# Mean over 8192 rows: paired loads up to row group 61, no early loads, the last group in pieces of 8, 4, 3 and 1 blocks, and 57 products on TensorE

## The chip, the cores and the metric

The kernel runs on one core of one Trainium2 chip. The metric is device time in microseconds (us): 628.41 us before the change, the median of three runs that lie between 628.18 and 628.45 us.

## The reference

```python
x = np.random.randn(8192, 8192).astype(np.float32)
return np.mean(x, axis=0)
```

The input is 8192 rows of 8192 floats, 268.4 MB in HBM. The result is one row of 8192 column means, 32 KB. Every input element is read once and enters one sum.

## The kernel before

**Tiling.** 128 rows make a row group (`G` = 64 groups, numbered 0 to 63), one row to a partition, 4 MB each. A row group has 16 blocks of `F` = 512 columns. One SBUF tile, `bufs`, holds six row groups: four are targets of loads, the fifth (`both`) and the sixth (`acc`) are used by the additions. Adding two row groups element by element keeps the 128 partial sums of a column apart, on 128 partitions; at the end TensorE sums over the partitions.

**Loading.** SyncE issues all loads (line 76), in program order, on one DMA queue. The first two loads of rows fetch groups 0 to 3 and 4 to 5; from group 6 to group 55 a load fetches two groups, so that each partition receives two neighbouring rows, 64 KB. From group 56 on a load fetches one group, 32 KB to a partition. A load into a buffer waits for the VectorE addition that read the buffer last. Two loads go ahead of their place (lines 111 and 113): blocks 14 and 15 of group 60 and blocks 9 to 13 of group 63 go to a tile of their own, `early`. GpSimd adds them into `acc` while the main loop runs (line 129), and the later loads of groups 60 and 63 leave these blocks out.

**Adding.** `add` (line 94) gives an addition to VectorE. Where an addition needs both a load and the addition before it, a no-op on ScalarE or GpSimd waits for the two, and the addition waits for the no-op. In the main loop there are two additions for a load: the pair is summed into `both`, and `both` is added to `acc`. Groups 56 to 59 are added to `acc` one by one. Of group 60 only blocks 0 to 13 are added on VectorE, of group 61 blocks 7 to 15. Three blocks of group 62 (14, 15 and 8) are added to `acc` by GpSimd (line 148).

**Summing over the partitions.** A product (line 183) multiplies a 128 x 32 tile filled with 1/8192 with a block of columns and accumulates in PSUM. It uses one of four 32-column parts of the TensorE array (`tile_position`, `q` = 0 to 3), so four products with different `q` can run side by side. What VectorE and GpSimd did not add goes to TensorE: blocks 0 to 6 of group 61, blocks 0 to 13 except 8 of group 62, and the 11 blocks of group 63 that were not loaded early, beside the 16 blocks of `acc`. With blocks that are spread over the four parts in pieces of 128, 160, 256 or 512 columns this makes 63 products. The order of the list `sums` is the order on TensorE.

**The end.** ScalarE copies four PSUM tiles to SBUF, VectorE copies the last one, and five stores write the result: two issued by ScalarE, three by SyncE. `landed` puts waits on SyncE; in the version before, they stand behind the last store.

What sets the order: each engine executes its own instructions in program order; engines wait for each other and for DMAs by semaphores.

Of the kernel before, what the change touches and what calls it, by code (L numbers as in the profile page):

```python
# [9 lines left out]
def kernel(  # L10
# [2 lines left out]
    x: bass.AP,  # L13
    out: bass.AP,
):

    nc = tc.nc
    f32 = mybir.dt.float32
    M, N = x.shape  # L40
    P = nc.NUM_PARTITIONS
    F = 512
    W = F // 4
    G = M // P
    U = 6
    sync = mybir.DependencyInfo(mybir.DependencyClass.Sync, mybir.DependencyReason.DATA)

    sb = ctx.enter_context(tc.tile_pool(name="sb", bufs=1))
    psp = ctx.enter_context(tc.tile_pool(name="psum", bufs=1, space=bass.MemoryType.PSUM))
# [2 lines left out]
    both = bufs[:, U - 2, :]  # L52
    acc = bufs[:, U - 1, :]
    ones = sb.tile([P, 32], f32, name="ones")
    early = sb.tile([P, 7 * F], f32, name="early")
    tail = sb.tile([P, W], f32, name="tail")
    warm = sb.tile([P, 32], f32, name="warm")
    nc.gpsimd.memset(ones[:], 1.0 / M)  # L58
    ready = sb.tile([P, 1], f32, name="ready")
    tc.keep_in_program_order(  # L60
        nc.gpsimd.tensor_add(out=ready[:], in0=ones[:, 0:1], in1=ones[:, 1:2]))  # L61
    banks = [psp.tile([P, F], f32, name=f"bank{b}") for b in range(2)]
    wide = psp.tile([P, 2 * F], f32, name="wide")
    two = psp.tile([P, 2 * W], f32, name="two")
    last = psp.tile([P, W], f32, name="last")

    loads = []

    def landed(*inss):

        nop = tc.keep_in_program_order(nc.sync.nop()).ins
        for o in inss:
            tc.add_manual_dep(nop, o.name, sync, reason="SyncE waits")

    def load(dst, src):
        ins = tc.keep_in_program_order(nc.sync.dma_start(out=dst, in_=src)).ins  # L76
        k = len(loads)
        over = loads[k - 8:k - 6] if k >= 8 and k % 2 == 0 else []
        tc.declare_no_dep(ins, group="loads", keep=over, reason="the reader of the buffer waited")
        for o in over:  # L80
            tc.add_manual_dep(ins, o.name, sync, reason="covers the next load too")
        tc.add_to_no_dep_group("loads", ins)
        loads.append(ins)
        return ins

    def rows(g, n=1):
        return x[g * P:(g + n) * P, :]

    def load_rows(g, u, n):
        return load(bufs[:, u:u + n, :], rows(g, n).rearrange("(p j) c -> p j c", j=n))  # L90
# [2 lines left out]

    def add(dst, a, b, dmas):

        ins = nc.vector.tensor_add(out=dst, in0=a, in1=b).ins  # L96
        if dmas and adds:
            waiter = nc.scalar if len(adds) % 8 > 1 else nc.gpsimd
            nop = joins[waiter] = tc.keep_in_program_order(waiter.nop()).ins  # L99
            for o in dmas + adds[-1:]:  # L100
                tc.add_manual_dep(nop, o.name, sync, reason="the no-op waits")
            for group in ("loads", "adds"):
                tc.declare_no_dep(ins, group=group, reason="the no-op waited")
            tc.add_manual_dep(ins, nop.name, sync, reason="waits for both at once")
        elif adds:
            tc.declare_no_dep(ins, group="loads", reason="the add ahead waited")
        tc.declare_no_dep(ins, group="early", reason="the no-op waited, or the add behind it")
        tc.add_to_no_dep_group("adds", ins)
        adds.append(ins)

    load(early[:, 5 * F:], rows(G - 4)[:, 14 * F:])
    first, second = load_rows(0, 0, 4), load_rows(4, 4, 2)
    load(early[:, :5 * F], rows(G - 1)[:, 9 * F:14 * F])
    add(bufs[:, 2:4, :], bufs[:, 2:4, :], bufs[:, 0:2, :], [first])
    add(bufs[:, 4:6, :], bufs[:, 4:6, :], bufs[:, 2:4, :], [second])
    add(acc, acc, both, [])
    tc.keep_in_program_order(nc.scalar.copy(out=warm[:], in_=ones[:]))  # L117
    ahead = []
    g = 6
    while g < G - 8:  # L120
        u = (g + 2) % 4
        dma = load_rows(g, u, 2)
        add(both, bufs[:, u, :], bufs[:, u + 1, :], [dma])
        add(acc, acc, both, ahead)
        ahead = []
        if g in (24, 32):
            lo, hi = (0, 4) if g == 24 else (4, 7)
            cols = slice((9 + lo) * F, (9 + hi) * F)
            ins = tc.keep_in_program_order(nc.gpsimd.tensor_add(  # L129
                out=acc[:, cols], in0=acc[:, cols], in1=early[:, lo * F:hi * F])).ins  # L130
            tc.add_to_no_dep_group("early", ins)
            ahead = [ins]
        g += 2

    while g < G - 4:
        row = bufs[:, (g + 2) % 4, :]
        add(acc, acc, row, [load(row, rows(g))])
        g += 1
    for lo, hi, loaded in [(0, 14, 14), (7, 16, 16)]:
        row = bufs[:, (g + 2) % 4, :]  # L140
        dma = load(row[:, :loaded * F], rows(g)[:, :loaded * F])
        cols = slice(lo * F, hi * F)
        add(acc[:, cols], acc[:, cols], row[:, cols], [dma])
        g += 1
    r61, r62, r63 = [bufs[:, (g + 1 + j) % 4, :] for j in range(3)]
    load(r62, rows(g))
    for cols in [slice(14 * F, 16 * F), slice(8 * F, 9 * F)]:
        joined = tc.keep_in_program_order(nc.gpsimd.tensor_add(  # L148
            out=acc[:, cols], in0=acc[:, cols], in1=r62[:, cols])).ins
    g += 1  # L150
    for lo, hi in [(4, 8), (0, 4), (14, 16), (8, 9)]:
        load(r63[:, lo * F:hi * F], rows(g)[:, lo * F:hi * F])

    sums = []

    def blocks(row, lo, hi):
        for i in range(lo, hi):
            sums.append((banks[i // 4], i % 4, 0, row[:, i * F:(i + 1) * F]))

    def spread(dst, row, lo, hi, part=slice(None)):  # L160
        n = (hi - lo) * W
        for c in range(0, n, F)[part]:
            for q in range(4):
                at = lo * F + q * n + c
                sums.append((dst, q, c, row[:, at:at + min(F, n - c)]))

    blocks(acc, 2, 5)
    blocks(acc, 0, 2)
    blocks(r61, 0, 7)
    blocks(acc, 5, 8)  # L170
    blocks(r62, 0, 8)
    spread(wide, acc, 9, 14, slice(1))
    blocks(r63, 4, 8)
    spread(wide, r62, 9, 14, slice(1))
    for row in (acc, r62):
        spread(wide, row, 9, 14, slice(1, 2))
    spread(two, acc, 14, 16)
    blocks(r63, 0, 4)
    spread(last, acc, 8, 9)
    spread(two, r63, 14, 16)  # L180
    spread(last, r63, 8, 9)
    for n, (dst, q, c, cols) in enumerate(sums):
        summed = tc.keep_in_program_order(nc.tensor.matmul(  # L183
            out=dst[32 * q:32 * q + 32, c:c + cols.shape[1]],
            lhsT=ones[:],
            rhs=cols,
            start=all((d is dst, k, at) != (True, q, c) for d, k, at, _ in sums[:n]),
            stop=all((d is dst, k, at) != (True, q, c) for d, k, at, _ in sums[n + 1:]),
            tile_position=(0, 32 * q),
            skip_group_check=True,  # L190
        )).ins

    res = both[:, :2 * F].rearrange("p (b c) -> p b c", b=2)
    res5 = both[:, 2 * F:2 * F + 5 * W]
    res2 = both[:, 4 * F:4 * F + 2 * W]

    def copy(dst, src):
        return tc.keep_in_program_order(nc.scalar.copy(out=dst, in_=src)).ins  # L198

    def store(engine, dst, src, *then):  # L200
        ins = tc.keep_in_program_order(engine.dma_start(out=dst, in_=src)).ins
        for o in then:
            tc.add_manual_dep(ins, o.name, sync, reason="follows that load")
        return ins

    def part(lo, hi):
        return out[lo * F:hi * F].rearrange("(q c) -> q c", q=4)

    copy(res[:, 1, :], banks[1][:])
    s1 = store(nc.scalar, part(4, 8), res[0:P:32, 1, :], loads[-4])  # L210
    copy(res5, wide[:, :5 * W])
    copy(res[:, 0, :], banks[0][:])
    copied = copy(res2, two[:])
    ended = nc.vector.tensor_copy(out=tail[:], in_=last[:]).ins  # L214
    landed(*joins.values())
    s5 = store(nc.sync, part(9, 14), res5[0:P:32, :], *loads[-7:-3])
    s0 = store(nc.sync, part(0, 4), res[0:P:32, 0, :])
    s2 = store(nc.scalar, part(14, 16), res2[0:P:32, :])
    store(nc.sync, part(8, 9), tail[0:P:32, :])
    landed(loads[-2], joined)  # L220
    landed(loads[-1], copied)
    landed(s0, s5)
    landed(s1, summed)
    landed(s2, ended)
    hold = tc.keep_in_program_order(nc.vector.nop()).ins
    tc.add_manual_dep(hold, s0.name, sync, reason="VectorE ends late")

# [29 lines left out]
```

## Time and profile before

| | |
|---|---|
| median of three runs | 628.41 us |
| span of the profiled execution, first to last instruction | 626.4 us |
| VectorE busy | 529.3 us (85%), 60 instructions |
| TensorE busy | 13.3 us (2%), 126 records for 63 products |
| GpSimd busy | 12.0 us (2%) |
| ScalarE busy | 3.7 us (1%) |
| HBM read | 268.44 MB, 429 GB/s over the span |

For the profiled execution only the span is given; its device time is taken to be the span plus 2.0 us, so that it stands at the median of the runs shown.

The profile has engine rows (PE is TensorE, PEld its weight loads, DVE is VectorE, ACT is ScalarE, POOL is GpSimd, SP is SyncE). An engine name with a q, such as SPq, is that engine's sequencer, which issues DMAs and waits. A line "out<-in" names what is written and read. [...]

### The profile page before, as it was taken

To read this page: it belongs to the slowest core of one execution; us is meant where nothing else is said; L and a number is where in the kernel's file an instruction comes from. 1 tells how busy PE (TensorE), PEld (TensorE's weight loads), DVE (VectorE), ACT (ScalarE), POOL (GpSimd) and SP (SyncE) were. 2 spreads that over 40 slices of the span, in tenths; PEclk is the share of its full clock that TensorE was granted. 3 is DMA by queue.
4 is the path that set the end of the run, shared out by engine and by line. 5 is a ranking of instruction groups with operands and counts; after the bars stand their busy time and mean duration, and the time that the engine had idled before them with its cause. 6 is when DMAs were issued, how large, how long until landed. Compare 5 with 4: busy or idle time off the path is not lost.

```text
span 626.4 us, 484 instructions
## 1 busy us (share of the span) xinstructions
PE 13.3 (2%) x126; PEld 4.0 (1%) x126; DVE 529.3 (85%) x60; ACT 3.7 (1%) x6; POOL 12.0 (2%) x10
## 2 busy tenths in 40 slices
PE   0000000000000000000000000000000000000008
PEld 0000000000000000000000000000000000000002
DVE  0028999998888998889998899888898888999992
ACT  0000000000000000000000000000000000000001
POOL 0000000000000000020000200000000000000002
PEclk9999999999999999999999999999999999999999
DMA  8999999999999999999999999999999999999997
GB/s 372 465 402 428 459 410 460 402 469 402 469 402 469 402 469 402 469 402 469 402 465 406 439 431 427 444 410 460 402 469 402 469 402 469 402 435 435 419 435 305
DMA packets 5930, 268.50 MB, mean 429 GB/s; under 512 B 660, under 2 KB 668, under 8 KB 1064
## 3 DMA queue, kind: packets, MB, share of 16 engines
q1 hardware_dynamic: 5912, 268.46, 99.3%
q8 instruction: 1, 0.02, 0.0%
q10 hardware_dynamic: 16, 0.01, 0.0%
q14 instruction: 1, 0.01, 0.0%
HBM read 268.44 MB, written 0.03 MB: 429 GB/s over the span
## 4 chain that ended last, share of the span: by engine, by line
DMA 59%; DVE 30%; another core or an unknown queue 10%; issue 0%; SPq 0%; ACTq 0%; PE 0%; POOL 0%; POOLq 0%
DMA bufs<-in_x_dram 59%; DVE bufs L96 30%; SPq L76 0%; ACTq L99 0%; PE last L183 0%; DVE tail L214 0%; POOL ready L61 0%; POOL ones L58 0%; POOLq L99 0%; POOLq L241 0%
## 5 line engine op out<-in xcount | busy, mean ns | idle before, releaser
L96 DVE TENSOR_TENSOR bufs<-bufs 128x8192 f32<-128x8192 f32 (+3 forms) x59 | 529.0, 8966 | 85.9 <-DMA bufs<-in_x_dram 43.0
L183 PE MATMUL bank<-bufs,ones 128*32 128x512 f32 x62 | 10.0, 716 | 610.3 <-DVE bufs L96 610.0
L129 POOL TENSOR_TENSOR bufs<-bufs,early 128x2048 f32<-128x2048 f32 (+1 forms) x2 | 7.9, 3954 | 348.5 <-DVE bufs L96 348.5
L148 POOL TENSOR_TENSOR bufs<-bufs 128x1024 f32<-128x1024 f32 (+1 forms) x2 | 3.6, 1824 | 258.9 <-DMA bufs<-in_x_dram 258.9
L214 DVE COPY tail<-last 128x128 f32<-128x128 f32 x1 | 0.3, 291 | 8.8 <-PE last L183 8.8
L183 PEld LDWEIGHTS bank<-bufs,ones 128*32 128x32 f32 x62 | 2.2, 121 | 616.4 <-issue 614.5
L198 ACT COPY bufs<-bank 128x512 f32<-128x512 f32 x2 | 1.2, 586 | 617.9 <-PE bank L183 617.9
L183 PE MATMUL wide<-bufs,ones 128*32 128x512 f32 (+1 forms) x32 | 2.5, 432 | 0.0
L117 ACT ACT_TABLE_LOAD x1 | 1.3, 1283 | 0.7 <-PEq L241 0.7
L183 PE MATMUL two<-bufs,ones 128*32 128x256 f32 x16 | 1.2, 380 | 0.0
L183 PEld LDWEIGHTS wide<-bufs,ones 128*32 128x32 f32 x32 | 1.0, 110 | 1.8 <-issue 1.8
L183 PE MATMUL last<-bufs,ones 128*32 128x128 f32 x16 | 0.8, 279 | 0.1
L198 ACT COPY bufs<-wide 128x640 f32<-128x640 f32 x1 | 0.7, 692 | 1.1 <-PE wide L183 1.1
L183 PEld LDWEIGHTS last<-bufs,ones 128*32 128x32 f32 x16 | 0.4, 109 | 1.2 <-issue 0.6
L183 PEld LDWEIGHTS two<-bufs,ones 128*32 128x32 f32 x16 | 0.4, 109 | 0.1
L198 ACT COPY bufs<-two 128x256 f32<-128x256 f32 x1 | 0.4, 372 | 0.1
L117 ACT COPY warm<-ones 128x32 f32<-128x32 f32 x1 | 0.2, 217 | 0.0
L61 POOL TENSOR_TENSOR ready<-ones 128x1 f32<-128x1 f32 x1 | 0.2, 193 | 0.1
L58 POOL MEMSET ones<- 128x32 f32 x1 | 0.1, 125 | 0.3 <-POOLq L241 0.3
L241 POOL MEMSET const-float32-0.0<- 128x1 f32 x1 | 0.1, 98 | 0.2 <-issue 0.2
L241 POOL MEMSET const-bfloat16-1.0<- 128x1 bf16 x1 | 0.1, 102 | 0.0
L241 POOL MEMSET const-uint8-127<- 128x1 uint8 x1 | 0.1, 102 | 0.0
(1 smaller groups left out, 0.1 us busy)
## 6 DMA issues: line engine op xcount, KB each, us to landing
bufs<-in_x_dram SPq DMA_DIRECT2D x6, 4096.0 KB, 20.4
bufs<-in_x_dram SPq DMA_DIRECT2D x1, 3584.0 KB
bufs<-in_x_dram SPq DMA_DIRECT2D x2, 1024.0 KB, 18.7
early<-in_x_dram SPq DMA_DIRECT2D x1, 1280.0 KB
early<-in_x_dram SPq DMA_DIRECT2D x1, 512.0 KB
bufs<-in_x_dram SPq DMA_DIRECT2D x1, 512.0 KB, 19.4
bufs<-in_x_dram SPq DMA_DIRECT2D x27, 29.9
bufs<-in_x_dram SPq DMA_DIRECT2D x1, 256.0 KB, 19.7
```

The source lines that it names most:

```text
L58: nc.gpsimd.memset(ones[:], 1.0 / M)
L61: nc.gpsimd.tensor_add(out=ready[:], in0=ones[:, 0:1], in1=ones[:, 1:2]))
L96: ins = nc.vector.tensor_add(out=dst, in0=a, in1=b).ins
L117: tc.keep_in_program_order(nc.scalar.copy(out=warm[:], in_=ones[:]))
L129: ins = tc.keep_in_program_order(nc.gpsimd.tensor_add(out=acc[:, cols], in0=acc[:, cols], in1=early[:, lo * F:hi * F])).ins
L148: joined = tc.keep_in_program_order(nc.gpsimd.tensor_add(out=acc[:, cols], in0=acc[:, cols], in1=r62[:, cols])).ins
L183: summed = tc.keep_in_program_order(nc.tensor.matmul(out=dst[32 * q:32 * q + 32, c:c + cols.shape[1]], lhsT=ones[:], rhs=cols, start=all(( ...
L198: return tc.keep_in_program_order(nc.scalar.copy(out=dst, in_=src)).ins
L214: ended = nc.vector.tensor_copy(out=tail[:], in_=last[:]).ins
L241: nc = _bacc.Bacc("TRN2", target_bir_lowering=False, num_devices=1)
```

## The change

The two early loads and their tile go, and with them the two GpSimd additions in the main loop. The first load now fetches groups 0 and 1, straight into `both` and `acc`, and every load up to that of groups 60 and 61 fetches two groups: 31 loads of 8 MB. Groups 60 and 61 are added to `acc` whole, by six VectorE additions over blocks 0 to 7, 8 to 11 and 12 to 15. Groups 62 and 63 are not added by VectorE or GpSimd at all: TensorE sums them. Group 62 is one load; group 63 comes in four loads of 8, 4, 3 and 1 blocks. TensorE makes 57 products: for `acc`, group 62 and group 63 each 15 of 512 columns, and the block 15 of each is spread over the four parts in pieces of 128 columns. ScalarE makes four copies (the fourth of 96 partitions), VectorE copies the last tile. There are three stores: blocks 0 to 11 by SyncE, blocks 12 to 14 by ScalarE, block 15 by SyncE. SyncE's waits for the loads, for the last ScalarE copy and for the last product now stand ahead of the last store instead of behind it.

```diff
-    early = sb.tile([P, 7 * F], f32, name="early")
...
-    banks = [psp.tile([P, F], f32, name=f"bank{b}") for b in range(2)]
-    wide = psp.tile([P, 2 * F], f32, name="wide")
-    two = psp.tile([P, 2 * W], f32, name="two")
+    banks = [psp.tile([P, F], f32, name=f"bank{b}") for b in range(4)]
...
-    load(early[:, 5 * F:], rows(G - 4)[:, 14 * F:])
-    first, second = load_rows(0, 0, 4), load_rows(4, 4, 2)
-    load(early[:, :5 * F], rows(G - 1)[:, 9 * F:14 * F])
-    add(bufs[:, 2:4, :], bufs[:, 2:4, :], bufs[:, 0:2, :], [first])
-    add(bufs[:, 4:6, :], bufs[:, 4:6, :], bufs[:, 2:4, :], [second])
-    add(acc, acc, both, [])
+    add(acc, acc, both, [load_rows(0, U - 2, 2)])
...
-    while g < G - 8:
+    for g in range(2, G - 4, 2):
         u = (g + 2) % 4
...
-    while g < G - 4:
-        row = bufs[:, (g + 2) % 4, :]
-        add(acc, acc, row, [load(row, rows(g))])
-        g += 1
-    for lo, hi, loaded in [(0, 14, 14), (7, 16, 16)]:
...
-    for lo, hi in [(4, 8), (0, 4), (14, 16), (8, 9)]:
-        load(r63[:, lo * F:hi * F], rows(g)[:, lo * F:hi * F])
+    u = (G - 4 + 2) % 4
+    dma = [load_rows(G - 4, u, 2)]
+    for lo, hi in [(0, 8), (8, 12), (12, 16)]:
+        cols = slice(lo * F, hi * F)
+        for j in range(2):
+            add(acc[:, cols], acc[:, cols], bufs[:, u + j, cols], dma)
+            dma = []
+    r62, r63 = [bufs[:, 2 - u + j, :] for j in range(2)]
+    load(r62, rows(G - 2))
+    for lo, hi in [(0, 8), (8, 12), (12, 15), (15, 16)]:
+        load(r63[:, lo * F:hi * F], rows(G - 1)[:, lo * F:hi * F])
...
+            if i < 15:
+                sums.append((banks[i // 4], i % 4, row[:, i * F:(i + 1) * F]))
+            else:
+                for q in range(4):
+                    at = i * F + q * W
+                    sums.append((last, q, row[:, at:at + W]))
...
+    blocks(acc, 0, 8)
+    blocks(r62, 0, 16)
+    blocks(acc, 8, 12)
+    blocks(r63, 0, 8)
+    blocks(r63, 8, 12)
+    blocks(acc, 12, 16)
+    blocks(r63, 12, 15)
+    blocks(r63, 15, 16)
...
+    for b in range(3):
+        copy(res[:, b, :], banks[b][:])
+    copied = copy(res[:96, 3, :], banks[3][:96])
     ended = nc.vector.tensor_copy(out=tail[:], in_=last[:]).ins
     landed(*joins.values())
+    s0 = store(nc.sync, out[:12 * F].rearrange("(b q c) -> q b c", q=4, c=F), res[0:P:32, 0:3, :])
+    s3 = store(nc.scalar, out[12 * F:15 * F].rearrange("(q c) -> q c", q=3), res[0:96:32, 3, :])
+    landed(loads[-5], set_up)
+    landed(*loads[-4:-2])
+    landed(loads[-2], copied)
+    landed(loads[-1], summed)
+    store(nc.sync, out[15 * F:].rearrange("(q c) -> q c", q=4), tail[0:P:32, :])
+    landed(s0, ended)
+    landed(s3)
```

More of the change, by code (lines that the diff above doesn't have):

```diff
@@ L59 @@
     ready = sb.tile([P, 1], f32, name="ready")
-    tc.keep_in_program_order(
-        nc.gpsimd.tensor_add(out=ready[:], in0=ones[:, 0:1], in1=ones[:, 1:2]))
-    banks = [psp.tile([P, F], f32, name=f"bank{b}") for b in range(2)]
-    wide = psp.tile([P, 2 * F], f32, name="wide")
-    two = psp.tile([P, 2 * W], f32, name="two")
+    set_up = tc.keep_in_program_order(
+        nc.gpsimd.tensor_add(out=ready[:], in0=ones[:, 0:1], in1=ones[:, 1:2])).ins
+    banks = [psp.tile([P, F], f32, name=f"bank{b}") for b in range(4)]
     last = psp.tile([P, W], f32, name="last")
@@ L94, in add @@
     def add(dst, a, b, dmas):
-        ins = nc.vector.tensor_add(out=dst, in0=a, in1=b).ins
+        ins = tc.keep_in_program_order(nc.vector.tensor_add(out=dst, in0=a, in1=b)).ins
         if dmas and adds:
@@ L106, in add @@
             tc.declare_no_dep(ins, group="loads", reason="the add ahead waited")
-        tc.declare_no_dep(ins, group="early", reason="the no-op waited, or the add behind it")
         tc.add_to_no_dep_group("adds", ins)
         adds.append(ins)
-    load(early[:, 5 * F:], rows(G - 4)[:, 14 * F:])
-    first, second = load_rows(0, 0, 4), load_rows(4, 4, 2)
-    load(early[:, :5 * F], rows(G - 1)[:, 9 * F:14 * F])
-    add(bufs[:, 2:4, :], bufs[:, 2:4, :], bufs[:, 0:2, :], [first])
-    add(bufs[:, 4:6, :], bufs[:, 4:6, :], bufs[:, 2:4, :], [second])
-    add(acc, acc, both, [])
+    add(acc, acc, both, [load_rows(0, U - 2, 2)])
     tc.keep_in_program_order(nc.scalar.copy(out=warm[:], in_=ones[:]))
-    ahead = []
-    g = 6
-    while g < G - 8:
+    for g in range(2, G - 4, 2):
         u = (g + 2) % 4
@@ L123 @@
         add(both, bufs[:, u, :], bufs[:, u + 1, :], [dma])
[L124 to L133, printed above, removed]
-    while g < G - 4:
-        row = bufs[:, (g + 2) % 4, :]
-        add(acc, acc, row, [load(row, rows(g))])
-        g += 1
-    for lo, hi, loaded in [(0, 14, 14), (7, 16, 16)]:
-        row = bufs[:, (g + 2) % 4, :]
-        dma = load(row[:, :loaded * F], rows(g)[:, :loaded * F])
-        cols = slice(lo * F, hi * F)
[L143 to L150, printed above, removed]
-    for lo, hi in [(4, 8), (0, 4), (14, 16), (8, 9)]:
-        load(r63[:, lo * F:hi * F], rows(g)[:, lo * F:hi * F])
+        add(acc, acc, both, [])
+    u = (G - 4 + 2) % 4
+    dma = [load_rows(G - 4, u, 2)]
+    for lo, hi in [(0, 8), (8, 12), (12, 16)]:
+        cols = slice(lo * F, hi * F)
+        for j in range(2):
[5 more added lines that the diff above has]
+        load(r63[:, lo * F:hi * F], rows(G - 1)[:, lo * F:hi * F])
     sums = []
@@ L157, in blocks @@
         for i in range(lo, hi):
[L158 to L182, printed above, removed]
+            if i < 15:
[12 more added lines that the diff above has]
+    blocks(r63, 15, 16)
+    for n, (dst, q, cols) in enumerate(sums):
         summed = tc.keep_in_program_order(nc.tensor.matmul(
-            out=dst[32 * q:32 * q + 32, c:c + cols.shape[1]],
+            out=dst[32 * q:32 * q + 32, :],
             lhsT=ones[:],
             rhs=cols,
-            start=all((d is dst, k, at) != (True, q, c) for d, k, at, _ in sums[:n]),
-            stop=all((d is dst, k, at) != (True, q, c) for d, k, at, _ in sums[n + 1:]),
+            start=all((d is dst, k) != (True, q) for d, k, _ in sums[:n]),
+            stop=all((d is dst, k) != (True, q) for d, k, _ in sums[n + 1:]),
             tile_position=(0, 32 * q),
@@ L191, with store @@
         )).ins
-    res = both[:, :2 * F].rearrange("p (b c) -> p b c", b=2)
-    res5 = both[:, 2 * F:2 * F + 5 * W]
-    res2 = both[:, 4 * F:4 * F + 2 * W]
+    res = both[:, :4 * F].rearrange("p (b c) -> p b c", b=4)
     def copy(dst, src):
         return tc.keep_in_program_order(nc.scalar.copy(out=dst, in_=src)).ins
[L200 to L213, printed above, removed]
+    def store(engine, dst, src):
+        return tc.keep_in_program_order(engine.dma_start(out=dst, in_=src)).ins
+    for b in range(3):
+        copy(res[:, b, :], banks[b][:])
+    copied = copy(res[:96, 3, :], banks[3][:96])
     ended = nc.vector.tensor_copy(out=tail[:], in_=last[:]).ins
     landed(*joins.values())
[L216 to L224, printed above, removed]
+    s0 = store(nc.sync, out[:12 * F].rearrange("(b q c) -> q b c", q=4, c=F), res[0:P:32, 0:3, :])
[7 more added lines that the diff above has]
+    landed(s3)
     hold = tc.keep_in_program_order(nc.vector.nop()).ins
```

## The prediction

> **What bounds the kernel now.** I read the page's slices first, then the chain that ended last, then the last 25 us as timeline and windows, because the change alters mostly the ends of the stream.
>
> ```profile
> DVE  0028999998888998889998899888898888999992
> DMA  8999999999999999999999999999999999999997
> ```
>
> The DMA row is full nearly throughout; VectorE has gaps. The chain of waits says the same: two VectorE additions, then a wait for a load, again and again, and at the end:
>
> ```profile
> 123.72 0.03 ACTq L99
> ...
> 162.42 0.03 ACTq L99
> ...
> 549.44 0.04 ACTq L99
> ...
> 603.45 19.74 DMA bufs<-in_x_dram
> 623.19 0.04 issue
> 623.23 0.47 PE last L183 x8
> 623.70 0.02 issue
> 623.73 0.29 DVE tail L214
> ```
>
> A line is start, duration, what. From 123.72 to 162.42 four row groups land: 38.70 us, 9.675 us a group. That is the stream's pace, and VectorE needs two additions of 8.70 us for two groups (17.4 of 19.35 us). So two things set the time: how long the stream takes, and what is left when it ends (623.19 to 626.4, 3.2 us). The timeline of TensorE and the stores (start, busy, what, count of records):
>
> ```profile
> 609.98 6.01 PE L183 MATMUL bank<-bufs,ones 128*32 128x512 f32 x30 [609.98 <-DVE bufs L96]
> 616.28 1.92 PE L183 MATMUL bank<-bufs,ones 128*32 128x512 f32 x16 [0.28 <-DMA bufs<-in_x_dram]
> 620.60 1.07 ACTq L201 DMA_DIRECT2D out_dram<-bufs  x1
> 623.63 0.51 ACTq L201 DMA_DIRECT2D out_dram<-bufs  x1
> 624.04 0.50 SPq L201 DMA_DIRECT2D out_dram<-tail  x1
> ```
>
> And the windows (stretch, length, PE busy, PE weight loads, VectorE, ScalarE, GpSimd, granted clock, DMA share, GB/s):
>
> ```profile
> 609.90:613.40 3.50, 3.42 (x16) 0.79 (x17) 3.46 (x1) 0.00 (x0) 0.00 (x0) 1.00 1.04 449
> 616.20:618.00 1.80, 1.72 (x16) 0.55 (x20) 0.00 (x0) 0.00 (x0) 1.51 (x1) 1.00 1.02 423
> 616.00:623.20 7.20, 6.88 (x88) 2.51 (x88) 0.00 (x0) 1.86 (x3) 3.61 (x2) 1.00 0.91 371
> ```
>
> Two things are to be seen. TensorE has hardly any idle time from 616 to 623.2: 6.88 of 7.20 us. And its first 16 records of 512 columns took 3.42 us, 16 later ones 1.72 us, although the clock column says 1.00 for both. The records start in fours, one for each part of the array: every 0.857 us at first, every 0.43 us later. I call this a beat; a product of 512 columns takes its part of the array two beats. The first 3.5 us of TensorE's work run at half pace.
>
> **The change, part by part.**
>
> *Start.* The early loads go. Offsets of landings against the pace: the first load (4.125 groups with the early blocks) landed at 42.99, 3.08 us above 4.125 x 9.675. At 123.72, with 12.4375 groups, the offset is 3.39. The load of five early blocks lies between and goes with about 0.28. The two-block load ahead of the first one is not separable: between 0 and the 0.45 us that SyncE issued the big load later (0.74 and 1.19 us). I take 0.03, since data flowed from the first issue on. VectorE's first addition starts some 20 us sooner, and the two additions that ran beside GpSimd's (11.21 and 10.12 instead of 8.70 us in the chain) become shorter; both lie under the stream, which left VectorE 1.9 us idle for each load. A load is issued when the addition of its buffers ends, 8.7 us after a landing, with 10.6 us of the other load in flight: this cover stays with pairs.
>
> *Groups 0 to 61.* 62 x 9.675 = 599.85, plus 3.05: the pair 60/61 lands at 602.9. Loads of single groups cost 9.72 (from 549.44 to 616.25, 6.875 groups in 66.8 us: 9.717), 0.04 more each; only group 62 is left of them, so it lands at 612.62. Group 63: before, four pieces of 11 blocks took 616.25 to 623.19, 6.94 us against 6.65 by the pace, 0.29 for four pieces. Now 16 blocks in four pieces: 9.68 + 0.28. Landings by size: blocks 0 to 7 at 617.5, 8 to 11 at 620.0, 12 to 14 at 621.9, block 15 at 622.6. The stream ends 0.6 us sooner than before (623.19).
>
> *VectorE at the end.* Groups 60 and 61 are added after 602.9 by six additions. From 8192 columns at 8.70 and 4608 at 4.96 us, a column costs 1.044 ns; 4096 columns 4.42 and 2048 columns 2.28 us, with 0.02 between. Blocks 0 to 7 of acc are ready at 602.96 + 8.88 = 611.84, 8 to 11 at 616.4, 12 to 15 at 621.0. All before the stream ends.
>
> *TensorE.* It starts at 611.9 instead of 609.98, since it waits for these additions, and it has more behind that point: of the 57 products each of the parts 0, 1 and 2 gets 12 of 512 and 3 of 128 columns, that is 24 long beats and 6 short ones of 0.109. By order on part 0: two products of acc in four slow beats, 611.9 + 3.43 = 615.33; four of group 62, to 618.76; a short one, 618.98; acc, 619.83; two of group 63, 621.55; one, 622.41; acc and a short one, 623.48; group 63, 624.34; the last short one, 624.56, and 0.16 until its result is there: 624.72. Each input is ready before its turn (group 62 at 612.62 for 615.33; acc 8 at 616.4 for 618.98; group 63 at 617.5 for 619.83, 620.0 for 621.55, 621.9 for 623.48, 622.6 for 624.34). So TensorE never waits for a load: it becomes the bound of the last 13 us and ends 2.1 us after the stream, where it ended 0.47 us after it. GpSimd's 3.6 us of additions of group 62 go, hidden before too.
>
> [...]
>
> *Copies and stores.* Bank 3 gets its last product 0.22 us before TensorE's end: 624.50. ScalarE's copy of 512 columns (0.586, after 0.07) ends at 625.16. The ScalarE store waits for it, issued at 625.19. What its issue costs is bounded by two rows: 1.07 us for the first store of that queue (2 KB pieces, loads in flight), 0.51 for the second (1 KB pieces, none in flight). The new store is the first and only one of its queue and has 2 KB pieces: I take 1.07. SyncE's waits ahead of the last store now include this copy: 625.19, one more wait of 0.06, then the last store at 625.3 instead of at 625.1, which is what VectorE's copy (624.79 to 625.08) would allow: 0.2 us. The 12-piece store, issued at 623.25, costs SyncE 0.51 (a four-piece row) to three times 0.64 us; even then it ends at 625.2 and is hidden. That cover is thin: 0.1 us.
>
> *The end.* Before, the span ended 2.25 us after the second ScalarE issue ended (624.14) and 1.85 us after the last SyncE issue ended (624.54). Now: 625.19 + 1.07 = 626.26 plus 1.85 to 2.25, I take 2.15 (two waits fewer follow): 628.4. By SyncE: 625.8 + 1.85 = 627.65. The larger holds: span 628.4, 2.0 more than 626.4. The profiled execution's time is taken at the runs' median, so 628.41 + 2.0 = 630.4.
>
> **Rivals.**
>
> *The store's issue is cheap.* With 0.51 the end is 627.85: 629.9. For it: the loads in flight at 620.6, gone by 625. Against: it is the queue's first.
>
> *The clock rises later.* Half pace for 3.5 us rests on one start. Every further us at half pace costs 0.5: one more stretch of 3.4 us gives 632.1. For it: TensorE starts from the same long idleness at another moment. Against: nothing in before shows another delay.
>
> *The stream is not shorter.* If what the small loads seemed to cost was there anyway, the pair 60/61 lands 0.6 later and all else with it: 631.0.
>
> *The other side: TensorE runs at full pace from its first product.* Then 1.7 us fall away, it ends at 623.0, 0.4 after the stream, and the stream's gain shows. With the cheap store: copy ends 623.46, last store 623.6 to 624.1, span 625.95, so 627.95; with the dear one 628.7. It decides from about 1 us saved on TensorE. Against: the doubled beat in the window from 609.90.
>
> **How the numbers follow.** Forecast 0.42; cheap store 0.25; later clock 0.14; no shorter stream 0.09; full pace 0.06; a stream shorter by another 0.4 (629.6 to 630.0) 0.04. A measurement can tell 0.2% (1.26 us) from no change: slower begins at 629.67. The forecast, the later clock and the unshortened stream lie above; the cheap store, at 629.9, mostly. Full pace lies within or, with luck, near the lower bound. So faster 0.03, same 0.17, slower 0.80. The range leaves out full pace and the far end of the later clock: 629.2 to 631.8.
>
> **What would show it.** TensorE's records without gaps from about 611.9 to 624.7, the last load landing near 622.5, VectorE's additions over by 621.1, the chain's end running through TensorE beats, the ScalarE copy and its store rather than through a load. If the chain still reaches a DMA wait just before the last four products, the TensorE step is wrong. If the ScalarE issue is near 0.5 us, the store step is.

## The result, and the profile after

The changed kernel takes 631.84 us (median of five runs, 631.49 to 632.18), the kernel before 628.29 (628.06 to 628.45): a ratio of 1.0056, 95% interval 1.0043 to 1.0068. It is slower, as forecast, by 3.55 us where 2.0 were forecast; the time lies 0.04 us above the end of the range, 631.8. The profiled execution of the changed kernel has a span of 629.6 us and belongs to the quickest of the five runs, 631.49.

The chain of waits of the changed kernel, its end (start, duration, what):

```profile
604.09 0.03 ACTq L74
604.12 0.03 issue
604.15 4.44 DVE bufs L71
608.58 0.02 issue
608.61 4.43 DVE bufs L71
613.04 0.09 issue
613.13 6.56 PE bank L125 x41
...
620.63 3.58 PE bank L125 x32
...
625.39 0.63 PE bank L125 x3
626.02 0.02 issue
626.05 0.58 ACT bufs L138
```

In the kernel before, a load stood in the chain until 623.19, and behind it only 0.47 us of TensorE and a copy of 0.29. Here no load stands in it after 604.09: two additions, TensorE without a break for 12.9 us, a ScalarE copy. The windows of the changed kernel (length, PE busy and records, then the other engines, clock, DMA):

```profile
613.00:616.50 3.50, 3.37 (x16) 0.90 (x20) 3.46 (x3) 0.00 (x0) 0.00 (x0) 1.00 1.03 440
619.40:626.20 6.80, 6.80 (x78) 3.12 (x71) 2.66 (x2) 1.91 (x4) 0.00 (x0) 1.00 0.40 157
```

Sixteen records need 3.4 us at first, as before. The weight loads, which go ahead of the records in fours, show where the pace doubles:

```profile
615.67 0.22 PEld L125 LDWEIGHTS bank<-bufs,ones 128*32 128x32 f32 x4 [0.63 <-issue]
616.52 0.22 PEld L125 LDWEIGHTS bank<-bufs,ones 128*32 128x32 f32 x4 [0.63 <-issue]
617.22 0.14 PEld L125 LDWEIGHTS bank<-bufs,ones 128*32 128x32 f32 x4 [0.48 <-issue]
617.65 0.14 PEld L125 LDWEIGHTS bank<-bufs,ones 128*32 128x32 f32 x4 [0.29 <-issue]
```

They start 0.85 us apart, then 0.70, then 0.43: the half pace is there again and ends near 617. In the last window TensorE is busy 6.80 of 6.80 us while the DMA share has fallen to 0.40: the stream has ended beneath it. The stores in the timeline:

```profile
626.66 1.28 ACTq L141 DMA_DIRECT2D out_dram<-bufs  x1
626.91 0.56 SPq L141 DMA_DIRECT2D out_dram<-tail  x1
```

One thing was in nobody's sum. VectorE in the middle of the stream:

```profile
448.52 17.42 DVE L71 TENSOR_TENSOR bufs<-bufs 128x8192 f32<-128x8192 f32 x2 [1.92 <-ACTq L74]
468.68 17.42 DVE L71 TENSOR_TENSOR bufs<-bufs 128x8192 f32<-128x8192 f32 x2 [2.73 <-ACTq L74]
488.02 8.69 DVE L71 TENSOR_TENSOR bufs<-bufs 128x8192 f32<-128x8192 f32 x1 [1.93 <-ACTq L74]
```

Before each pair of additions VectorE waits 1.9 us for the load; once it waits 2.73 us. From 429.19 to 448.52 there are 19.33 us, from 448.52 to 468.68 there are 20.16: one landing is 0.8 us late, and every later one stays as late. In the window from 462.2 to 463.2 us the DMA view has

```profile
q14 instruction: 1, 0.01, 2.1%
```

and the same view of the kernel before, from 300 to 500 us, has the load queue alone:

```profile
q1 hardware_dynamic: 1472, 85.98, 99.3%
```

One packet of 8 KB of instructions, at 462.33 us by the trace's packet records, 0.33 us long. A load of two groups is 128 packets of 64 KB, 2.42 us each. Eight of them for each of the 16 DMA engines make 19.36 us, which is the pace of two groups (19.35), and from 100 to 600 us 16 packets are in flight 98% of the time; each 64 KB packet starts within 0.012 us of the end of another. So every DMA engine has an equal share of a load and no idle time in which to catch up. The 64 KB packet that begins as the instruction packet ends takes 3.08 instead of 2.42 us: its engine loses 0.33 + 0.66 = 0.99 us. That engine's last packet of the load ends at 468.15, the last of the 15 others at 467.36, and the landing waits for the slowest: 0.8 us of the loss shows there.

Against the kernel before, the spans differ by 3.2 us (629.6 and 626.4). The last load lands at 623.66 instead of 623.19: 0.47. TensorE's last result comes 2.56 us after it (626.22) instead of 0.47: 2.09. From there to the end of the span 3.38 instead of 2.73: 0.65. Another 0.35 us lies between the profiled run and the median.

### The profile page after: what moved, and what is told of

Same layout as the page of the kernel before. It is cut to its first block, busy times and chain, and to the rows that moved or that the text cites. A ratio compares the mean times of both kernels' runs of the same rounds, so it can differ in the third digit from the quotient of the medians.

```text
span 629.6 us, 442 instructions
## 1 busy us (share of the span) xinstructions
PE 13.1 (2%) x114; PEld 4.9 (1%) x114; DVE 531.0 (84%) x66; ACT 3.8 (1%) x6; POOL 0.5 (0%) x6
## 4 chain that ended last, share of the span: by engine, by line
DMA 67%; DVE 21%; another core or an unknown queue 9%; PE 2%; ACT 0%; issue 0%; ACTq 0%
DMA bufs<-in_x_dram 67%; DVE bufs L71 21%; PE bank L125 2%; ACT L86 0%; PE last L125 0%; ACT bufs L138 0%; ACTq L74 0%; ACT warm L86 0%
## 5 line engine op out<-in xcount | busy, mean ns | idle before, releaser
L71 DVE TENSOR_TENSOR bufs<-bufs 128x8192 f32<-128x8192 f32 (+2 forms) x65 | 530.7, 8167 | 91.4 <-ACTq L74 43.3
L125 PE MATMUL bank<-bufs,ones 128*32 128x512 f32 x90 | 12.8, 687 | 613.1 <-DVE bufs L71 613.1
L125 PEld LDWEIGHTS bank<-bufs,ones 128*32 128x32 f32 x90 | 4.2, 125 | 619.3 <-issue 618.2
L138 ACT COPY bufs<-bank 128x512 f32<-128x512 f32 (+1 forms) x4 | 2.3, 584 | 622.0 <-DMA bufs<-in_x_dram 620.2
L125 PE MATMUL last<-bufs,ones 128*32 128x128 f32 x24 | 2.3, 276 | 0.0
```

The source lines that it names most:

```text
L71: ins = tc.keep_in_program_order(nc.vector.tensor_add(out=dst, in0=a, in1=b)).ins
L125: summed = tc.keep_in_program_order(nc.tensor.matmul(out=dst[32 * q:32 * q + 32, :], lhsT=ones[:], rhs=cols, start=all((d is dst, k) != (T ...
```

## The experiments

Theory: TensorE bounds the last 13 us, from its first real product on; half pace at its start and the dear ScalarE store count fully; what lands late shifts all of it. Rival: the end is set by the loads and stores, and TensorE's lateness only follows. A second question is where the instruction packet came from.

**Products ahead (e1_warm).**

```diff
+    junk = psp.tile([P, F], f32, name="junk")
...
+    for i in range(28):
+        q = i % 4
+        tc.keep_in_program_order(nc.tensor.matmul(
+            out=junk[32 * q:32 * q + 32, :],
+            lhsT=ones[:],
+            rhs=bufs[:, u, (i % 16) * F:(i % 16 + 1) * F],
...
+        ))
     for n, (dst, q, cols) in enumerate(sums):
```

> The changed kernel with 28 products of group 60 added ahead of the real ones, into a PSUM tile that nobody reads; they can run from the landing of groups 60 and 61 (604.1 us in the changed kernel's profile), 9 us before the first real product. Theory (TensorE bounds the last 13 us, and its first 3.9 us at half pace count): the real products still start at 613.1 but 43 beats of 0.43 us follow at once, so TensorE ends 1.9 us sooner, near 624.3 instead of 626.2, and the time falls by 1.9 us to 629.9. Rival (the end is set by the last loads and the stores, TensorE only follows): TensorE ends sooner or not, the time stays at 631.8 within 0.3.

Measured 630.16 us (629.82 to 630.78), 1.68 less than the changed kernel; ratio to the kernel before 1.0031 (1.0019 to 1.0044). The timeline of this run:

```profile
604.36 8.87 PE L127 MATMUL junk<-bufs,ones 128*32 128x512 f32 x56 [604.36 <-DMA bufs<-in_x_dram]
613.22 4.92 PE L137 MATMUL bank<-bufs,ones 128*32 128x512 f32 x43
...
622.28 0.15 PEld L137 LDWEIGHTS bank<-bufs,ones 128*32 128x32 f32 x6 [0.76 <-DVE bufs L72]
...
623.86 0.16 PEld L137 LDWEIGHTS last<-bufs,ones 128*32 128x32 f32 x5 [0.35 <-DMA bufs<-in_x_dram]
```

The real products begin at the same time (613.22, before 613.13) and end at 624.64 instead of 626.22, 1.58 sooner; the span is 1.58 shorter (628.02). So of the 1.9 us forecast 1.58 show in the span. The rest went to the last two lines: now that TensorE is quicker, its weight loads wait for VectorE's last additions and then for the last loads.

**Products more (e9_eight_more).**

```diff
     for n, (dst, q, cols) in enumerate(sums):
+        if n == 27:
+            for i in range(8):
+                tc.keep_in_program_order(nc.tensor.matmul(
+                    out=junk[32 * (i % 4):32 * (i % 4) + 32, :],
+                    lhsT=ones[:],
+                    rhs=r62[:, i * F:(i + 1) * F],
...
+                ))
```

> The changed kernel with eight products more, two for each part of the TensorE array, in the middle of its work (behind those of group 62), on blocks of group 62 that have landed, into a PSUM tile that nobody reads. Theory (TensorE bounds from its first product to the end): four beats of 0.43 us are added, all of it shows: 631.84 + 1.72 = 633.6. Rival (TensorE has slack behind the last loads, or the stores set the end): less than 0.5 us is added, 631.8 to 632.3.

Measured 633.37 us (632.52 to 634.43): 1.53 more. The added records stand in the chain itself:

```profile
620.04 1.72 PE junk L128 x15
621.76 3.58 PE bank L137 x33
```

In the profiled execution TensorE takes 1.30 us longer than in the changed kernel: 1.72 added, and 0.4 less because its half pace was 0.8 us shorter this time. Added work shows nearly whole, and so does removed half pace: TensorE is the bound there, and the rival falls.

**A DMA early on ScalarE (e2_queue).**

```diff
+    prime = sb.tile([4, F], f32, name="prime")
...
     tc.keep_in_program_order(nc.scalar.copy(out=warm[:], in_=ones[:]))
+    tc.keep_in_program_order(nc.scalar.dma_start(out=prime[:], in_=x[0:4, 0:F]))
```

> The changed kernel with one small DMA more: ScalarE loads 4 x 512 floats into a tile that nobody reads, right after its first copy at 2 us. Theory (the first DMA that ScalarE issues is dear, 1.28 us here and 1.07 us before, later ones about 0.55): the store's issue at the end falls from 1.28 to about 0.55 us; the time falls by 0.3 us only, since the last store on SyncE, which lands at about the same moment, is next in line: 631.5. Rival (the issue is dear by its shape, 3 pieces of 2 KB from 96 partitions): it stays near 1.28 us and the time at 631.8.

Measured 631.68 us (631.38 to 632.0), not to be told from 631.84. The issues on ScalarE:

```profile
0.90 0.55 ACTq L88 DMA_DIRECT2D prime<-in_x_dram  x1
...
626.98 0.78 ACTq L143 DMA_DIRECT2D out_dram<-bufs  x1
```

The store's issue fell from 1.28 to 0.78 us, not to 0.55; and the very first DMA of that queue cost 0.55 only. So "the first is dear" does not hold as put. With the early DMA the store's issue takes 0.78 us here; without it, it takes 1.28 in the changed kernel, e1_warm and e9_eight_more. So the early DMA made the later issue cheaper; what the rest is made of stays open. It is worth little here, since the SyncE store lands at about the same time.

**The first load cut in two (e3_small_first).**

```diff
-    add(acc, acc, both, [load_rows(0, U - 2, 2)])
+    two_rows = rows(0, 2).rearrange("(p j) c -> p j c", j=2)
+    first = [load(bufs[:, U - 2:, :2 * F], two_rows[:, :, :2 * F]), load(bufs[:, U - 2:, 2 * F:], two_rows[:, :, 2 * F:])]
+    add(acc, acc, both, first)
```

> The changed kernel with its first load cut in two: blocks 0 and 1 of the two groups first (4 KB to a row, 1 MB), then blocks 2 to 15 (28 KB to a row). Theory (a small load ahead lines up the DMA engines, so the early load of the kernel before shortened the start): the first landing comes 0.2 to 0.35 us sooner than 22.76, all later landings as well, time 631.5. Rival (the start costs the same, the offset of 0.35 us came from something else): landing at 22.7 to 23.0, time 631.8 to 632.1.

Measured 632.63 us (631.98 to 632.91), 0.8 more than the changed kernel at the median, though the runs of the two overlap. VectorE's first addition waits until 24.09 instead of 22.79:

```profile
24.09 8.69 DVE L71 TENSOR_TENSOR bufs<-bufs 128x8192 f32<-128x8192 f32 x1 [24.09 <-DMA bufs<-in_x_dram]
```

The cut costs 1.3 us at the start. Not all of it is left at the end, since the instruction packet made the landings of this run only 0.17 us late (the pairs of additions around it begin at 449.78 and 469.30, 19.52 us apart instead of 19.35). Neither theory nor rival had that: the small pieces ahead of the paired load were no gain here.

**The early load alone (e7_early).**

```diff
+    early = sb.tile([P, 2 * F], f32, name="early")
...
+    load(early[:], rows(G - 4)[:, 14 * F:])
     add(acc, acc, both, [load_rows(0, U - 2, 2)])
```

> The changed kernel with the kernel before's first load put in front again (blocks 14 and 15 of group 60, 128 rows of 4 KB), but only loaded, into a tile that nobody reads; so 0.5 MB is moved twice, which by the pace costs 1.21 us. Theory (this load lines up the DMA engines at the start): groups 0 and 1 land at 22.76 + 1.21 - 0.33 = 23.64. Rival (it is an ordinary load and its cost is its bytes): 23.97. With the three-edit run's cut load, which landed 1.2 us late, a third outcome is a landing near 25.

A single run, 631.97 us. The pair landed at 23.70, near the theory's 23.64. But the first landing of kernels with the same start varies from run to run: 22.76 in the changed kernel, 22.65, 22.52 and 22.55 in e1_warm, e8_six_more_after and e9_eight_more. Less its own 1.21 us this one has 22.49. So the early load's gain at the start is 0 to 0.3 us and not settled.

**The three together (e4_three).** The edits of e1_warm, e2_queue and e3_small_first.

> The three edits of the runs beside it together: products ahead at the landing of groups 60 and 61, a small DMA issued early by ScalarE, the first load cut in two. Theory: the gains add up, since they lie one behind the other on the path: 1.9 + 0.3 + 0.3, and with the sooner end the store's cheap issue counts fully: 629.2. Rival: they cover each other and the loads' end holds the kernel at about 630.5.

Measured 630.83 us (630.76 to 631.37), not the 629.2 of the theory: the 1.7 us of the products ahead, less about 0.8 us for the cut load. The rival's 630.5 is near, and part of its reason holds: the chain of this run goes through a load again (blocks 8 to 11 of group 63, landed at 622.34), for which TensorE waits 0.67 us.

**Six VectorE instructions more, in the kernel before (e5_six_more).**

```diff
     warm = sb.tile([P, 32], f32, name="warm")
+    tiny = sb.tile([P, 8], f32, name="tiny")
+    for i in range(6):
+        tc.keep_in_program_order(nc.vector.memset(tiny[:, i:i + 1], 0.0))
```

> The kernel before with six tiny VectorE instructions more at its head (memsets of one column of a tile that nobody reads), so that VectorE has 74 instructions in its program, as many as in the changed kernel, instead of 68. In the changed kernel one 8 KB instruction packet was fetched at 462.3 us, in the middle of the stream, and from the next landing on all loads are 0.82 us late; in the kernel before there is none until its last store is out. Theory (the fetch is the next piece of VectorE's program, and comes when VectorE has got so far): such a packet appears between 390 and 470 us, one landing interval is 0.1 to 1 us too long, and the time rises by as much, 628.4 to 629.3. Rival (the fetch has to do with something else of the changed kernel): no packet, 628.3 within 0.2.

Measured 629.11 us (628.95 to 629.34) against 628.13 (627.84 to 628.46) in the same comparison: ratio 1.0014 (1.0005 to 1.0023). Six instructions that together take 0.2 us, while VectorE waits for its first load anyway, cost 1 us. VectorE in this run:

```profile
413.94 17.42 DVE L99 TENSOR_TENSOR bufs<-bufs 128x8192 f32<-128x8192 f32 x2 [1.94 <-ACTq L102]
434.10 17.42 DVE L99 TENSOR_TENSOR bufs<-bufs 128x8192 f32<-128x8192 f32 x2 [2.75 <-ACTq L102]
```

and in the window from 427 to 429 us:

```profile
q14 instruction: 1, 0.01, 1.0%
```

The packet (427.77 us), the long wait, 0.8 us again.

**The same six in the changed kernel (e8_six_more_after).** The same edit.

> The changed kernel with the same six tiny VectorE instructions at its head. Theory of VectorE's program: the packet comes six additions sooner, 3 x 19.35 = 58 us before 462.3, so near 404 us, and the long landing interval with it. Rival: it stays at 462 us within 9 us. The time is near 631.8 in either case.

A single run, 631.55 us. The packet came at 404.07 us, and the long wait with it:

```profile
390.24 17.42 DVE L74 TENSOR_TENSOR bufs<-bufs 128x8192 f32<-128x8192 f32 x2 [1.93 <-ACTq L77]
410.41 17.42 DVE L74 TENSOR_TENSOR bufs<-bufs 128x8192 f32<-128x8192 f32 x2 [2.75 <-ACTq L77]
```

Six VectorE instructions more, six additions sooner. With and without the six, VectorE is then at the 47th of its recorded instructions, and so it is in every run here that has the packet in its stream.

**Two more (e10_two_more).** As e5_six_more, with two instead of six.

> The kernel before with two tiny VectorE instructions more, 70 in all; 68 had no instruction packet in the middle of the stream, 72 and 74 had one. Theory (a second piece of VectorE's program is fetched when the program is longer than some length, when VectorE reaches a fixed place in it): if 70 is over the length, a packet comes near 428 + 2 x 19.35 = 466 us with a landing up to 1 us late, and 628.4 to 629.2; if it isn't, there is none and 628.2 within 0.2. A packet at another time would speak against the fixed place.

Measured 629.13 us (628.69 to 629.66) against 628.27: ratio 1.0013 (1.0004 to 1.0023). The packet came at 466.6 us, the forecast being 466:

```profile
452.93 17.42 DVE L99 TENSOR_TENSOR bufs<-bufs 128x8192 f32<-128x8192 f32 x2 [1.94 <-POOLq L102]
472.95 17.42 DVE L99 TENSOR_TENSOR bufs<-bufs 128x8192 f32<-128x8192 f32 x2 [2.60 <-ACTq L102]
```

The kernel before has 68 VectorE instructions and no such packet during the stream (one comes at 626.03, behind the last store's issue); 70 bring it. Whether the number itself decides, or the place in memory that the program happens to get, was not tried apart; the changed kernel's 74 are on the far side.

**The head of the kernel before, without early loads (e6_head).**

```diff
-    add(acc, acc, both, [load_rows(0, U - 2, 2)])
+    first, second = load_rows(0, 0, 4), load_rows(4, 4, 2)
+    add(bufs[:, 2:4, :], bufs[:, 2:4, :], bufs[:, 0:2, :], [first])
+    add(bufs[:, 4:6, :], bufs[:, 4:6, :], bufs[:, 2:4, :], [second])
+    add(acc, acc, both, [])
...
-    for g in range(2, G - 4, 2):
+    for g in range(6, G - 4, 2):
```

> The changed kernel with the head of the kernel before, but for the early loads: first groups 0 to 3, then 4 and 5, three additions. VectorE has two instructions fewer (72). Theory of VectorE's program, if the fetch goes by the position in the program: the packet comes two instructions later for the same position, but the two skipped additions fall in the first groups, so by time it comes near 462 + 19 + 19 = 500 us less what the wide ones take over: 480 to 505. The start: if the two-block early load was what made it shorter, the offset of landings stays 3.4 us as in the changed kernel (groups 0 to 3 land at 42.1); if the load of four groups did, it is 3.1 (41.8). Time 631.5 to 631.9.

Measured 634.12 us (633.5 to 634.47), 2.3 more than the changed kernel and far outside the 631.5 to 631.9 expected. The packet came at 483 us, as expected, and this time delayed no landing, though the next 64 KB packet took 3.08 us again: its DMA engine was, it seems, far enough ahead of the slowest. Groups 0 to 3 landed at 41.91, between the two values put down, so the start is not settled by it. The loss is elsewhere. The third load is issued when the first, wide addition has freed its buffers:

```profile
59.19 54.75 SPq L51 DMA_DIRECT2D bufs<-in_x_dram  x4
61.32 69.79 DVE L71 TENSOR_TENSOR bufs<-bufs 128x16384 f32<-128x16384 f32 x7 [2.16 <-POOLq L74]
```

At 59.19 the second load has 2.1 us left, it lands at 61.26, and groups 6 and 7 land at 82.86, 21.60 us later instead of 19.35. The DMA engines ran dry: of 16 packets in flight, 6 are left at 60.8 us. In the kernel before, the early load of five blocks lies in that place, 3.0 us of data. That is what it did for the start of the kernel before; the changed kernel, with pairs from the first load on, has no need of it. This is not the whole account: another 0.8 us goes by the landing of groups 12 and 13, its cause open, and in the profiled execution the half pace lasted 5.5 instead of 3.9 us, another 0.8; the packet without effect gives 0.8 back.

No run here beats the kernel before. With the products ahead and without the packet, the changed kernel would be near 629.3, an estimate from these differences (630.16 less 0.9), still above 628.3; that was not built.

## Why the prediction was right or wrong

*Direction and main mechanism: right.* TensorE became the bound of the end. First product 9.04 us after the landing of groups 60 and 61 (forecast 9.0), no wait for a load in its work, the copy of bank 3 and the ScalarE store behind it, the chain without a load: all as put. e1_warm and e9_eight_more show it by taking from TensorE and adding to it.

*The step that failed: "The stream ends 0.6 us sooner than before."* It ended 0.47 later. The pair 60/61 was put at 602.9 and landed at 604.09, 1.19 late. Of that, about 0.8 is the instruction packet; the rest, about 0.4, is the start, which I took as 3.05 us above the pace and which was 3.41 (22.76 less 19.35). The rival "the stream is not shorter" named the right place, but put 0.6 us there, half of what came, and for another reason. That the change brings six more VectorE instructions was not counted in my sum, which put VectorE's additions under the stream at no cost; what they brought with them was an instruction packet that takes DMA time (0.33 us, and 0.66 at the next packet), and the DMA engines had none to spare. e5_six_more, e8_six_more_after and e10_two_more show this cause. The start stays open. By the packet records the first 64 KB packet of each DMA engine took 2.9 to 3.5 us in the changed kernel instead of 2.42; but in the kernel before the first packets, of 4 KB, were late as well (0.2 to 0.9 us instead of 0.16), and nothing here tells the two apart.

*Half pace.* Put at 3.5 us, it lasted 3.9 (613.13 to 617.06, where the packed trace's record of the granted clock begins): TensorE needed 13.09 us instead of 12.82. By the same records it was 3.1 us in e9_eight_more, 5.4 in e1_warm and 5.5 in e6_head. So no run shows that half pace comes in stretches of 3.4 us, as the rival "the clock rises later" priced it; what sets its length was not shown. Its spread is probably part of why the runs of the changed kernel spread over 0.7 us; the packet's delay, which also differs from run to run, may be another. Neither was measured over several runs of one kernel.

*The store.* Issue put at 1.07, measured 1.28; from its end to the end of the span put at 2.15, measured 1.66. Together 0.28 us less than forecast. The reason for taking the dear row (the queue's first) did not hold up in e2_queue.

*The sum again:* 628.4 of span, plus 1.19 landing, 0.04 start of TensorE, 0.27 half pace, less 0.28 store: 629.6, the span measured. The forecast time of 630.4 misses 631.84 by these 1.2 us and the 0.35 between the profiled run and the median, less 0.1 of what lies around the span.

*The range* reached to 631.8. It held the later clock and the unshortened stream each, but not a cost in the stream beyond "no gain", since the trace of before shows no instruction packet during the stream but one of 16 KB on queue 8 at 622.56, as the last loads land. It is no work of the change: the changed kernel has one too, at 623.07. In e1_warm it falls at 617.72, among the loads of group 63, and these land at the same distances as in the changed kernel within 0.03 us.

*What did not matter:* the 12-piece store (issued at 624.74, 0.69 us) stayed hidden; its cover is 1.5 us, not the 0.1 that I feared, since its issue cost little more than that of a four-piece store on SyncE (0.56 us).

## What to carry to other kernels

Work that is moved behind the last data is priced on the engine that does it, at the pace that this engine has at that moment: here TensorE started at half pace, and 28 unneeded products while it waited were worth 1.7 us. This stream kept all DMA engines full, each with eight packets of a load, and a single packet of 8 KB on one of them made every later landing up to 0.98 us late; so count instructions too, and look in the DMA view for queues that are not yours. When a load is taken out, ask what it covered, not only what it moved.

## What the runs showed of the hardware

A VectorE program of 68 instructions ran without an instruction packet on queue 14 during the stream; with 70, 72, 74 and more one of 8 KB came, while VectorE was at its 47th recorded instruction, and cost up to 1.0 us of a full stream (1 us of time in e5_six_more, 0.9 in e10_two_more). The loss is that of one DMA engine, 0.33 us for the packet and 0.66 for the next 64 KB packet, which took 3.08 instead of 2.42 us in each of the eleven runs. How much of it a landing shows differs: 0.98 us in e1_warm, 0.8 in the changed kernel, 0.42 in e2_queue, 0.17 in e3_small_first, nothing in e6_head.

ScalarE's DMA issue cost between 0.51 and 1.28 us for pieces of 1 and 2 KB: 1.07 (before) and 1.28 (after) for a first one at the end of the kernel, 0.55 for a first one at its start, 0.78 at the end with one 626 us before it (both in e2_queue), 0.51 with one 3 us before it (before).
